# A planned instruction order ranked by lateness over ten passes, with the second projection, the FFN products and the decode buffers moved

## The chip, the cores and the metric

The kernel runs on one core of one Trainium2 chip. The metric is the device time of one execution in microseconds (us), from the median of several runs. The core has five engines that work side by side: PE (matrix multiply; its weight loads are shown apart as PEld), DVE (vector), ACT (scalar and activation), POOL and SP. SP does no arithmetic here: it issues nearly all transfers. Each engine takes its instructions in the order in which the program holds them, and an instruction that waits for another engine holds up what is queued behind it.

## The reference

One step of a hybrid decoder layer, for a prompt of 1024 rows and 8 decode rows of width 1024, with shared weights:

```python
h = x + 0.5 * rmsnorm(swiglu(rmsnorm(x, g1), gate1, up1, down1), p1)   # FFN 1, inner width 2816
proj = rmsnorm(h, g2) @ w_in                  # 1024 -> 3328: q, k, v of group A, the rest group B
ya = diff_attention(q, k, v)                  # 4 heads x 2 maps of 64, causal; decode rows read 512 cached keys
yb, state = rwkv7_time_mix(pb)                # 8 heads of 64, a recurrent state, solved in chunks
h = h + rmsnorm(concat(ya, yb) @ w_out, p2)
h = h + 0.5 * rmsnorm(swiglu(rmsnorm(h, g3), gate2, up2, down2), p3)   # FFN 2
```

Outputs are h for prompt and decode rows, the keys and values, and the states.

## The kernel before, in words

**Tiling.** Rows are the free dimension (columns of the tiles), features lie on the 128 partitions. The 1032 rows are cut in two halves, half 0 with 520 rows (8 decode rows and 512 of the prompt) and half 1 with 512, and each half in two chunks of 256 or 264. Each weight tile is split into a high and a low part in the format fp32r (ACT makes the high part, POOL or DVE the low one), and each product takes three matmuls (`mm3`), high by high, high by low and low by high.

**Stages.** The trunk (`s_trunk`, L751 on) runs four phases: FFN 1 of half 0 (phase 0), FFN 1 of half 1 (phase 1), FFN 2 of half 0 (phase 2) and FFN 2 of half 1 (phase 3). A phase goes through 22 tiles of the inner width; for each tile f there is a gate product, an up product and elementwise work, and after every group of two or three f a down product is added into `y` (tile `xl0`). The activations of four f at most are kept in a ring (tile `xl1`), so after four f a phase cannot go on without a down product, and the first down product waits for `("tail", ph - 1, c)`, the signal that the earlier phase's `y` is read out. Weight tiles of the trunk have four places in phases 0 and 3, and two (`w0`, `w1`) in phases 1 and 2.

Per half, a chain of its own leads from one FFN to the next: `s_tail` (norm of `y`, the residual fetched two tiles at a time into the double buffer `hres`, the sum stored to `res`, its norm, and the input `px` of the projection), `s_project` (26 tiles of w_in), four jobs of the recurrent mixer (`s_job`, two side by side, with locks on shared tiles), `s_attend`, `s_out` (w_out), `s_outnorm` and `s_pre`, which makes the next FFN's input. The decode rows go through `a_decode` (64 gathers of cached pages, issued by POOL: 8 requests, 4 pages, keys and values) and `b_decode`.

**What waits for what around the change.** `s_project(1)` waits for `("outw", 0)`, the end of half 0's output projection. `s_mix(0)` waits for `dec_a` before the jobs may take their sets of tiles, because `a_decode` borrows two of them (`own`). Phase 2 can begin when `s_outnorm` and `s_pre` of half 0 are done, phase 3 when those of half 1 are.

**Order.** The steps are written as streams (generators) that hand in operations. `run` is a list scheduler at build time: it prices each operation with constants in the file (a transfer counts as landed 2.0 us after its bytes, the last line below), keeps a clock for each engine, and again and again takes an operation that can start earliest; among those that can start within 0.02 us of each other the smaller number of the stream's fixed priority (`PRIO`) goes first. On PE the trunk has 3, the projections 1, most others 0. The order so found is the order of the program.

```python
c.append((max(free[e], o.ready + o.load, held[OTHER[e]] if o.port else 0.0), st.prio[e], o))
...
o.seen = rings + 2.0
```

All operations pass through one helper (L277), so the profile tells them apart by their tiles: `trunk_m` is a trunk product, `proj_m` a projection's, `job_aux` and `job_dec` the mixer's, `attn_*` attention's, `out_m` and `outb_m` the output projections of halves 0 and 1, `tail_*` the step between FFN 1 and the projection.

## Time and profile before

| what | us |
|---|---|
| median of 3 runs (2528.1 to 2532.65) | 2532.31 |
| the profiled execution, its own time | 2543.23 |
| span of the profiled execution | 2541.5 |
| PE busy in it | 2368.8 |
| DVE, ACT, POOL busy | 1425.4, 1022.3, 1044.4 |
| mean clock granted to PE, share of full speed | 0.958 |

PE is busy for 93% of the span, no other engine for more than 56%. So the profile is read by stage: where PE is not busy, where its granted clock is under 1.00, and what it waited for there. The time between the profiled execution and its span is 1.7 us.

### The profile page before, as it was taken

Reading aid. Unit: us, or ns where it says so; the run is one execution under the profiler, and the core shown is the slowest. Engines: PE = TensorE matmul, PEld = TensorE weight load, DVE = VectorE, ACT = ScalarE, POOL = GpSimd, SP = SyncE. Lnnn points to the kernel's source line nnn. Section 1 sums busy time; section 2 is a strip of 40 time slices with the busy share of each in tenths; the row PEclk is TensorE's granted clock in tenths of the full one; section 3 lists DMA queues with packets and bytes.
Section 4 is the critical chain, followed back from the end, with each engine's and each line's share of the span. In section 5 each row is a group of like instructions: output and inputs, shape, how many; then the busy total and the mean of one; then the engine's idle time right before and its main releaser. Section 6 shows DMA issues by size and latency. Waiting matters only on the chain.

```text
span 2541.5 us, 41893 instructions
## 1 busy us (share of the span) xinstructions
PE 2368.8 (93%) x16149; PEld 2081.2 (82%) x16149; DVE 1425.4 (56%) x3058; ACT 1022.3 (40%) x1994; POOL 1044.4 (41%) x831
## 2 busy tenths in 40 slices
PE   7999997898999999998499999999999996999998
PEld 7999997698877777776387788989978996788887
DVE  5554444647778676567555367575467656432323
ACT  5632223422244433345444244433365555422223
POOL 4443333435544433355545333343433354322222
PEclk8999999898999999998599999999999998999999
DMA  5422334267653223495355433223444342533232
GB/s 183 130 86 89 92 93 133 73 181 215 195 157 96 84 64 85 111 215 146 96 155 153 141 108 84 80 74 93 107 128 129 112 146 63 157 93 98 88 96 76
DMA packets 455485, 299.14 MB, mean 118 GB/s; under 512 B 79311, under 2 KB 426547, under 8 KB 455286
## 3 DMA queue, kind: packets, MB, share of 16 engines
q1 hardware_dynamic: 449414, 277.55, 37.8%
q0 software_dynamic: 5584, 18.39, 2.4%
q8 instruction: 127, 2.08, 0.3%
q14 instruction: 72, 0.59, 0.1%
q10 hardware_dynamic: 288, 0.52, 0.1%
HBM read 254.91 MB, written 41.49 MB: 117 GB/s over the span
## 4 chain that ended last, share of the span: by engine, by line
PE 73%; DVE 10%; DMA 5%; ACT 5%; POOL 3%; issue 3%; SPq 1%; DVEq 0%; POOLq 0%; ACTq 0%
PE trunk_m L277 45%; PE proj_m L277 8%; PE job_aux L277 6%; PE trunk_aux L277 4%; PE attn_m L277 2%; PE attn_aux L277 2%; PE out_m L277 2%; PE outb_m L277 1%; PE job_dec L277 1%; DVE bset_solve L277 1%; DVE mix_T L277 1%; DVE trunk_xl L277 1%; ACT wts_w L277 1%; POOL wts_w L277 1%; DVE bset_bv L277 1%
## 5 line engine op out<-in xcount | busy, mean ns | idle before, releaser
L277 POOL TENSOR_TENSOR wts_w<-wts_raw,wts_w 128x1024 fp32r<-128x1024 f32 (+1 forms) x183 | 408.0, 2230 | 691.9 <-ACT wts_w L277 603.4
L277 PE MATMUL trunk_m<-pre_X,wts_w 128*128 128x256 f32 (+1 forms) x4224 | 561.7, 290 | 13.1 <-DVE trunk_g L277 8.2
L277 PEld LDWEIGHTS trunk_m<-pre_X,wts_w 128*128 128x128 f32 x4224 | 528.6, 192 | 26.8 <-DVE trunk_g L277 9.0
L277 PE MATMUL trunk_m<-trunk_xl,wts_w 128*128 128x264 f32 (+2 forms) x3105 | 511.4, 318 | 29.8 <-DVE trunk_xl L277 26.0
L277 PEld LDWEIGHTS trunk_m<-trunk_xl,wts_w 128*128 128x128 f32 x3105 | 436.7, 191 | 71.4 <-DVE trunk_xl L277 29.2
L277 PE MATMUL trunk_m<-pre_T,wts_w 128*128 128x512 f32 (+1 forms) x1944 | 453.3, 384 | 2.6 <-DVE wts_w L277 1.3
L277 ACT CAST wts_w<-wts_raw 128x1024 fp32r<-128x1024 f32 (+1 forms) x288 | 281.1, 976 | 392.1 <-PE trunk_m L277 291.9
L277 PEld LDWEIGHTS trunk_m<-pre_T,wts_w 128*128 128x128 f32 x1944 | 340.9, 190 | 75.5 <-issue 7.0
L277 DVE TENSOR_TENSOR trunk_xl<-trunk_xl,trunk_m 128x264 f32<-128x264 f32 (+2 forms) x330 | 158.5, 485 | 151.6 <-PE trunk_m L277 150.3
L277 PE MATMUL proj_m<-tail_X,lin_w 128*128 128x264 f32 (+1 forms) x1248 | 170.0, 296 | 9.7 <-DVE lin_w L277 4.6
L277 PEld LDWEIGHTS proj_m<-tail_X,lin_w 128*128 128x128 f32 x1248 | 162.0, 199 | 19.0 <-ACT tail_X L277 5.4
L277 DVE TENSOR_TENSOR wts_w<-wts_raw,wts_w 128x1024 fp32r<-128x1024 f32 (+1 forms) x105 | 125.5, 1196 | 51.4 <-ACT wts_w L277 50.2
L277 PE MATMUL proj_m<-tail_T,lin_w 128*128 128x512 f32 x624 | 149.3, 398 | 1.9 <-ACT lin_w L277 1.4
L277 PEld LDWEIGHTS proj_m<-tail_T,lin_w 128*128 128x128 f32 x624 | 116.6, 188 | 32.0 <-issue 2.8
L277 POOL TENSOR_TENSOR trunk_xl<-trunk_t,trunk_xl 128x264 fp32r<-128x264 f32 (+2 forms) x84 | 87.1, 1037 | 99.1 <-ACT trunk_xl L277 99.1
L277 DVE SCALAR_TENSOR_TENSOR trunk_g<-trunk_t,trunk_m 128x264 f32<-128x264 f32 (+2 forms) x86 | 45.4, 529 | 124.8 <-ACT trunk_t L277 124.3
L277 ACT CAST trunk_xl<-trunk_t 128x256 fp32r<-128x256 f32 (+2 forms) x136 | 63.8, 469 | 107.7 <-DVE trunk_t L277 67.9
L277 ACT ACTIVATE trunk_t<-trunk_m 128x264 f32<-128x264 f32 (+2 forms) x86 | 40.6, 472 | 142.7 <-PE trunk_m L277 135.7
L277 DVE TENSOR_TENSOR trunk_t<-trunk_g,trunk_m 128x264 f32<-128x264 f32 (+2 forms) x83 | 43.7, 526 | 83.5 <-PE trunk_m L277 78.6
L277 DVE TENSOR_TENSOR bset_solve<-job_LT,bset_solve 128x60 f32<-128x60 f32 (+24 forms) x248 | 80.0, 322 | 17.1 <-DMA job_LT<-Md 7.4
L277 PE MATMUL trunk_aux<-pre_T,wts_w 128*128 128x512 f32 (+1 forms) x360 | 78.9, 374 | 0.0
L277 POOL TENSOR_TENSOR lin_w<-lin_lraw,lin_w 128x1024 fp32r<-128x1024 f32 x20 | 49.2, 2458 | 72.3 <-ACT lin_w L277 61.7
(493 smaller groups left out, 3489.3 us busy)
## 6 DMA issues: line engine op xcount, KB each, us to landing
wts_raw<-in_ffn_gate_dram SPq DMA_DIRECT2D x88, 512.0 KB
wts_raw<-in_ffn_up_dram SPq DMA_DIRECT2D x88, 512.0 KB
wts_raw<-in_ffn_down_dram SPq DMA_DIRECT2D x96, 384.0 KB
lin_lraw<-in_w_in_dram SPq DMA_DIRECT2D x26, 512.0 KB
lin_LT<-in_w_in_dram SPq DMA_DIRECT2D x26, 512.0 KB
wts_raw<-in_ffn_down_dram SPq DMA_DIRECT2D x16, 512.0 KB
lin_lraw<-in_w_out_dram SPq DMA_DIRECT2D x12, 512.0 KB
lin_LT<-in_w_out_dram SPq DMA_DIRECT2D x12, 512.0 KB
```

The costliest lines, as they stand in the source:

```text
L277: o = Op(eng, lambda: fn(*a, **k), st)
```

## The change

The whole order is planned ten times without building it; after each pass `latest` places the operations backward from the planned end and so finds for each the latest start that would not move the end. In the next pass an engine that has several operations ready takes the one with the smallest such number, instead of the stream's priority. The pass with the earliest planned end is built.

Beside that the structure changes. `s_project(1)` no longer waits for half 0's output projection: it gets its own weight places in the tiles of `y` and of the ring (which phase 1 has left), and phase 2 takes these again only after `proj1`. In phase 0 `s_tail` writes its result to two stage tiles and not over `y`, and gives the signal `("tail", 0, c)` there; a new stream `s_resid` fetches the whole residual of a half before `s_tail` needs it, into one of the tiles that held the FFN's input, and these places then take the squares. `px` of chunk 0 now waits for the sums of chunk 1. The decode step has tiles of its own (room for them comes from a smaller `dynamic_dma_scratch_size`), so the jobs do not wait for `dec_a`; `s_out(0)` does. The projection of half 0 begins with the mixer's tiles; that of half 1 does its first two tiles by chunks. A trunk weight is fetched before its place is free, and only the split waits.

```diff
-PRIO = {"stats": (1, 1), "lin": (1, 1), "proj": (1, 1), "tail": (0, 0), "dec": (0, 0), "trunk": (-1, 3), "wts": (0, 0), "outb": (1, 1), "out": (0, 4)}
+PASSES = 10
+
+PRIO = {"stats": (1, 1), "lin": (1, 1), "proj": (1, 1), "tail": (0, 0), "dec": (1, 1), "job": (-2, 0), "trunk": (-1, 3), "wts": (0, 0), "outb": (1, 1), "out": (0, 0), "resid": (-2, 0)}
@@ run
-                        c.append((max(free[e], o.ready + o.load, held[OTHER[e]] if o.port else 0.0), st.prio[e], o))
+                        c.append((max(free[e], o.ready + o.load, held[OTHER[e]] if o.port else 0.0), st.prio[e] if o.late is None else o.late, o))
...
+    def latest(self):
+        late = [self.predicted] * len(self.ops)
+        gaps = {e: [(-1e9, self.predicted)] for e in ENGINES}
+        for i in sorted(range(len(self.ops)), key=lambda i: (self.ops[i].start, i), reverse=True):
+            o = self.ops[i]
+            g = gaps[o.eng]
...
+            t = late[i] = min(b, late[i]) - o.cost
...
+            if o.before is not None:
+                late[o.before] = min(late[o.before], t)
+            for j in o.deps:
+                d = self.ops[j]
+                late[j] = min(late[j], t - o.load - (self.after(d, o) - d.start) + d.cost)
+        return {o.key: t for o, t in zip(self.ops, late)}
@@ s_weights
-                if tag in last:
-                    yield ("wait", last[tag])
                 raw = self.raw()
...
                 nc.sync.dma_start(raw.rearrange("p (a b) -> p a b", a=a), src)
+                if tag in last:
+                    yield ("wait", last[tag])
@@ s_trunk
         for ph in range(4):
+            if ph % 2 == 0:
+                if ph:
+                    yield ("wait", "proj1")
+                y = self.T(self.big, [P, 4160], "xl0")
+                self.ytile, self.y = y, y.rearrange("p (k t) -> p k t", k=KT)
+                ring = self.T(self.big, [P, 4160], "xl1", FR)
@@ s_tail
-        self.post(acc, y, f"n_ffn{1 + ph // 2}_post", h0 + o)
+        z = rs = None
+        if ph < 2:
+            yield ("wait", ("resid", ph))
+            rs = self.rs[c][0]
+        if ph == 0:
+            if c == 0:
+                self.zt = self.stage()
+            z = [a + b for a, b in self.parts(half, *self.zt)][c]
+        self.post(acc, y, f"n_ffn{1 + ph // 2}_post", h0 + o, z, rs)
...
+            if z:
+                self.signal(("tail", ph, c))
...
+            for k in range(KT):
+                nc.scalar.activation(rs[k], y[k], AF.Square)
+                if k:
+                    self.either("tensor_tensor", rb if k > 1 else rb, rb if k > 1 else rs[0], rs[k], ALU.add, engines=("vector",))
+            yield
+            self.rstd(rb)
+            yield
             if c == 0:
+                yield ("wait", ("summed", ph))
                 self.px = self.parts(half, *self.two(half))
...
+            else:
+                self.signal(("summed", ph))
+                yield ("wait", ("px", ph, 0))
@@ new stream, spawned at the last up product of phases 0 and 1
+    def s_resid(self, ph):
+        half = ph % 2
+        yield ("wait", ("ups", ph))
+        yield ("wait", ("loaded", half))
+        t = self.T(self.pool, [P, 4160], f"{'XT'[half]}1")
+        self.rs = self.parts(half, t)
+        t = t.rearrange("p (k t) -> p k t", t=520)
+        for o, n in CHUNKS[half]:
+            a = HALVES[half][0] + o
+            for k in range(0, KT, 4):
+                self.nc.sync.dma_start(t[:, k:k + 4, o:o + n], self.res[:, k:k + 4, a:a + n])
+        self.signal(("resid", ph))
+        yield
@@ s_project
-        yield ("wait", ("outw", 0) if half else "w23")
+        places = None
+        if half:
+            raws, pairs = self.T(self.big, [P, 4160], "xl1"), self.T(self.big, [P, 4160], "xl0", FR)
+            places = [raws[:, 1024 * j:1024 * j + 1024] for j in range(4)], [pairs[:, 2048 * j:2048 * j + 2048] for j in range(2)]
+        else:
+            yield ("wait", "w23")
...
-            list(range(8)) + ms + list(range(8, 12)) + [m + i for i in range(1, 4) for m in job]
+            ms + [m + 1 for m in job] + list(range(8)) + [m + i for i in range(2, 4) for m in job] + list(range(8, 12))
...
-        units = [(i, c) for i in range(len(ms)) for c in ((2,) if half else range(2))]
+        units = [(i, c) for i in range(len(ms)) for c in ((2,) if half and i > 1 else range(2))]
@@ s_out
         if half == 0:
+            yield ("wait", "dec_a")
             yield ("wait", "dec_b")
@@ s_mix
-        if half == 0:
-            yield ("wait", "dec_a")
@@ s_rope
+        if half:
+            yield ("wait", ("outw", 0))
@@ a_decode
-        *self.pages, q0 = [heads(t) for t in [self.own[j][0].rearrange("p n t -> p (n t)") for j in range(2)] + [self.own[j][2] for j in range(2)]]
+        *self.pages, q0 = [heads(self.T(self.pool, [P, HS], f"page{j}")) for j in range(4)]
@@ kernel
-    nc = _bacc.Bacc("TRN2", target_bir_lowering=False, num_devices=1)
+        nc = _bacc.Bacc("TRN2", target_bir_lowering=False, num_devices=1, dynamic_dma_scratch_size=2048)
...
+    for _ in range(PASSES):
+        try:
+            build(late, True)
+        except Planned as p:
+            plans.append((p.args[0], len(plans), late))
+            late = p.args[1]
+    nc = build(min(plans, key=lambda p: p[:2])[2], False)
```

## Rows read from the trace of the kernel before

**Rows 1.** Page, busy us of each engine; and the chain that ended last, by engine.
```profile
PE 2368.8 (93%) x16149; PEld 2081.2 (82%) x16149; DVE 1425.4 (56%) x3058; ACT 1022.3 (40%) x1994; POOL 1044.4 (41%) x831
...
PE 73%; DVE 10%; DMA 5%; ACT 5%; POOL 3%; issue 3%; SPq 1%; DVEq 0%; POOLq 0%; ACTq 0%
```

**Rows 2.** Busy time by stage: window, its us, each engine, PEclk, DMA share, GB/s.
```profile
0.00:64.00 64.00, 48.18 (x326) 45.12 (x327) 32.64 (x64) 34.71 (x64) 31.78 (x34) 0.89 0.55 183
64.00:380.00 316.00, 313.70 (x2597) 312.28 (x2596) 148.54 (x292) 111.02 (x191) 123.77 (x103) 0.99 0.33 98
380.00:510.00 130.00, 104.15 (x647) 92.04 (x647) 68.35 (x110) 53.56 (x94) 52.11 (x55) 0.87 0.35 104
510.00:700.00 190.00, 171.88 (x1302) 164.25 (x1300) 124.50 (x238) 47.85 (x80) 92.47 (x82) 0.95 0.66 196
700.00:1144.00 444.00, 433.41 (x2702) 340.79 (x2702) 305.12 (x761) 183.49 (x372) 191.85 (x136) 0.98 0.44 116
1144.00:1336.00 192.00, 141.91 (x851) 120.18 (x851) 119.57 (x260) 91.17 (x213) 94.76 (x96) 0.80 0.46 133
1336.00:2096.00 760.00, 739.60 (x5657) 659.04 (x5656) 453.37 (x1086) 346.05 (x745) 312.18 (x221) 0.99 0.39 113
2096.00:2160.00 64.00, 43.50 (x306) 40.80 (x306) 43.37 (x71) 35.85 (x66) 29.27 (x34) 0.81 0.21 62
2160.00:2478.00 318.00, 317.28 (x1406) 256.33 (x1405) 105.73 (x139) 93.74 (x124) 97.36 (x57) 1.00 0.36 106
2478.00:2541.50 63.50, 55.16 (x375) 50.33 (x373) 24.20 (x46) 24.82 (x48) 18.88 (x17) 0.95 0.23 75
```

**Rows 3.** Timeline of PE, end of phase 0 [idle before, and its releaser].
```profile
414.78 0.67 PE L277 MATMUL tail_dec<-trunk_acc,init_onesD 128*128 128x264 f32 x2
415.10 7.04 PE L277 MATMUL trunk_m<-trunk_xl,wts_w 128*128 128x256 f32 x57
...
444.47 1.25 PE L277 MATMUL tail_dec<-init_prb,init_onesD 128*128 128x264 f32 x2 [16.01 <-DVE init_prb L277]
449.56 9.24 PE L277 MATMUL proj_m<-tail_X,lin_w 128*128 128x264 f32 x24 [3.84 <-ACT tail_X L277]
...
472.76 17.00 PE L277 MATMUL trunk_m<-pre_T,wts_w 128*128 128x512 f32 x72 [0.86 <-DVE wts_w L277]
```

**Rows 4.** Chain that ended last, inside that wait: start us, us, what.
```profile
429.33 1.15 DVE lin_w L277
430.50 0.37 SPq L277
430.92 4.42 DMA tail_hres<-res
```

**Rows 5.** Timeline of PE, from phase 1's end to the second projection.
```profile
1231.71 2.29 PE L277 MATMUL trunk_m<-trunk_xl,wts_w 128*128 128x256 f32 x9 [6.47 <-DVE trunk_xl L277]
...
1253.41 0.59 PE L277 MATMUL out_m<-out_X,lin_w 128*128 128x264 f32 x1 [15.21 <-ACT out_X L277]
...
1263.62 40.33 PE L277 MATMUL out_m<-out_X,lin_w 128*128 128x256 f32 x335 [0.34 <-DVE out_X L277]
1303.79 2.04 PE L277 MATMUL proj_m<-tail_T,lin_w 128*128 128x512 f32 x8
```

**Rows 6.** Timeline of DVE, last pieces of the second projection's input (tail_T).
```profile
1272.62 0.48 DVE L277 SCALAR_TENSOR_TENSOR tail_T<-tail_sq,setup_cols,tail_T 128x256 fp32r<-128x256 f32 x1 [1.18 <-ACT tail_T L277]
```

**Rows 7.** Page, costliest groups: the two projections (half 0, then half 1) on PE.
```profile
L277 PE MATMUL proj_m<-tail_X,lin_w 128*128 128x264 f32 (+1 forms) x1248 | 170.0, 296 | 9.7 <-DVE lin_w L277 4.6
L277 PE MATMUL proj_m<-tail_T,lin_w 128*128 128x512 f32 x624 | 149.3, 398 | 1.9 <-ACT lin_w L277 1.4
```

**Rows 8.** Timeline of PE, end of the second output projection, and phase 2's end.
```profile
2088.35 5.62 PE L277 MATMUL outb_m<-outb_T,lin_w 128*128 128x256 f32 x46
...
2140.81 9.07 PE L277 MATMUL trunk_m<-trunk_xl,wts_w 128*128 128x264 f32 x55 [14.28 <-DVE trunk_xl L277]
```

**Rows 9.** Chain that ended last, in the decode step: a gather of cached keys.
```profile
560.59 7.59 DMA bset_TT<-in_cache_k_dram,dec_ptab
```

## The prediction, made before the changed kernel ran

> **What bounds the kernel now.** I read the page's busy times and the engine shares of its chain first. PE is busy for 2368.8 us of 2541.5 and carries 73% of the chain; DVE, the next, is busy for 56% [rows 1]. So the kernel ends when PE has done its products, and time can come from three places only: fewer products, less idle time on PE, or less time at its lower clock. The change takes no product away, so I read the second view, busy time by stage, for the other two [rows 2]. Width less PE busy is the idle time of a stage: 15.8, 2.3, 25.9, 18.1, 10.6, 50.1, 20.4, 20.5, 0.7 and 8.3 us, in all 172.7. [...]

> Then I read the waits of PE inside the joints. At the end of phase 0 PE stood 16.01 us before one small product of the tail [rows 3]. The chain of waits says why: the residual's fetch was queued on SP behind a fetch of projection weights, which waited until DVE had split the tile before (429.33 to 430.48); then the fetch took 4.42 us to land [rows 4]. At the end of phase 1 PE stood 6.47 us for DVE, 15.21 us for the input of the output projection, and only at 1303.79, behind 40 us of it, did the second projection begin [rows 5], although the last pieces of its input were made from 1272.62 on [rows 6]. At the end of phase 2 PE stood 14.28 us for a DVE addition that empties its result [rows 8].

> **End of phase 0 (380 to 510): 20 us gained.** Removed: eight residual fetches through the double buffer, with SP's and POOL's share of the wait. Added: four larger fetches issued when the last up product is planned, so they land beside the last down products; the DMA engines are busy for 35% there [rows 2], which covers the same bytes moved earlier. If that cover fails, the fetch costs what it did, about 6 us from 429.33 to its landing at 435.34 [rows 4]. The tail of chunk 0 took from 414.78 to 449.56, 34.8 us [rows 3]; without those 6.0 it takes 28.8. Chunk 1 is some 7 us behind, the 7.04 of its last down products [rows 3], and now holds up the input of both (the wait on the sums): 414.8 + 7 + 28.8 = 451. The first 24 projection products, 3.3 us of work by [rows 7], took 9.24 behind the input's pieces [rows 3], so a chunk of input is worth some 9 us, and both are there by 469. Does PE have work until then? A phase 1 product of 512 columns takes 17.00/72 = 0.236 us [rows 3]; one inner tile has 48 of them, 11.3 us, and four tiles are allowed before the first down product: 45 us from 428 on, to 473. The first down product is allowed early too, since the result no longer lies in `y`. So the 16.0 and the 4.0 of clock go; of the other 9.8 us idle I give back nothing. Bounds: 0, if the wait on the sums puts the hole behind it; 29.9, if all of it goes. I take 20, near the row of the single wait that is named.

> **First projection and decode (510 to 700): 6 us.** The jobs no longer wait for the decode step, and the trunk's early down products can fill. The stage has 18.1 idle and 0.4 of clock, in small waits. No row shows the two side by side; bounds -10 (gathers that land late hold DVE, see the rival) and 18.5. I take a third. Added to it are seven small DVE operations for the decode sums; DVE is busy for 124.5 of 190 us [rows 2] and hides them. Four clears of tiles on POOL go and are worth nothing: POOL is busy for half the stage.

> **End of phase 1 (1144 to 1336): 50 us.** This is the main term. The second projection has 149.3 us of products [rows 7] and did not run while PE stood idle for 50.1 us and lost at least 13.4 to the clock; together 63.5. Its new places are in tiles that phase 1 leaves, so it waits for its own input alone. What is late next is that input: the tail of phase 1, 28.8 us by the count above, when trunk products have ended. Attention of half 0 is the work beside it, if the order keeps some of it until then; the backward plan should, since phase 1's end now heads the longer chain. I leave 13.5 of the 63.5 there. The added wait (phase 2 for `proj1`) has behind it only phase 2's own products, which need half 0's output projection anyway. The second projection's end then lies before the output projection's. Rope of half 1 now waits for that too; attention 1 is what reads it, hundreds of us later. Bounds: 0 and 63.5.

> **End of phase 2 (2096 to 2160): 8 us.** Nothing structural changes. The 14.28 us are an order on DVE and ACT: input of phase 3 ahead of an addition that PE needed [rows 8]. Ranking by the latest start may put the addition first, or move the wait to the input. Bounds 0 and 22.4 (20.5 + 1.9); I take about half of the wait.

> **Elsewhere: nothing.** Start and end (15.8, 8.3) keep their causes, and the stages 700 to 1144 and 1336 to 2096 stand at 97 to 98% PE. The trunk's weights are fetched sooner, with PE waiting for none of them long. Added products: two tiles of the second projection are done by chunks, 96 of 256 columns at 170.0/1248 = 0.136 us for 48 of 512 at 149.3/624 = 0.239 [rows 7], 13.1 - 11.5 = 1.6 us more.

> **Sum.** 20 + 6 + 50 + 8 - 1.6 = 82 us. The profiled execution, 2543.2 with 1.7 outside its span, would come to 2461; the median shown stands 10.9 lower, at 2532.3, so I predict 2450.

> **Rivals.** [...]

> Second, half 1's chain has a length of its own. From its first product at 1303.79 to the last of the output projection at 2094.0 [rows 5, 8] it took 790 us, through four jobs with locks. If PE did not set that, the chain can begin only as early as its input: about 1276 [rows 6], less the 26 us from the first two joints, so 1250, 54 us sooner. Then the gain is 54, at 2480. For it: the trunk fills PE there, at low priority, so that a full PE proves no bound. Against it: with phase 1 ranked ahead of attention its input comes earlier than 1250.

> Third, slower: gathers in order queues. A decode gather on the chain took 7.59 us to land [rows 9]; the order counts 2.0 us after the bytes, so a planned use can be some 5 us early. Now the jobs run beside them with nothing between, and the DVE and POOL instructions behind a late gather are job steps and trunk additions. The 64 gathers at 5 us are 320 us of held queues. The gain is lost when a quarter of it (82/320) reaches PE; at a half the kernel takes 2532 - 82 + 160 = 2610. Against it: with the same gathers beside the first projection PE lost 18.1 us in all [rows 2], and three are in flight at once. [...]

> That the ranking does nothing is possible too, since the first of the ten orders is by fixed priorities and may win: without the 8 and the 6 the time is 2464, inside the forecast.

> **How the numbers follow.** Forecast (2425 to 2475) 0.55; own chain (2475 to 2510) 0.20; clock (2385 to 2425) 0.12; a gain that late landings just eat, 0.04; slower by them, 0.09. A measurement of this kernel tells 0.2% from no change, about 5 us. The range 2400 to 2515 holds the first two and most of the third; it leaves out 0.16. Faster 0.87, same 0.04, slower 0.09.

> **What would show it.** In the changed profile: no wait over 5 us on the residual at the end of phase 0, second-projection products before the first output projection's, and an idle share in the window that answers to 1144 to 1336 of under 20 us. The second rival shows as idle PE before phase 3 with jobs or attention as releasers; the third as gathers releasing DVE or POOL in PE's waits. The prediction is wrong in its main term if PE still stands idle between phase 1's last down product and the second projection.

## The result and the profile after

| | before | after |
|---|---|---|
| median, us | 2532.48 | 2503.59 (4 runs, 2500.17 to 2505.41) |
| ratio, 95% interval | 1 | 0.9877 [0.9859, 0.9896] |
| span of the profiled execution | 2541.5 | 2500.1 |

The change gains 29 us by the medians and 41 by the two profiled spans; the 12 between are the two executions' own, since the profiled one of before lay 10.8 us over its median and that of after 1.6 under. Ratios here and below are of undisturbed executions: e1 had two slow ones, of 2659.26 and 3785.03 us, that its median counts and its ratio does not. 2450 was forecast, a gain of 82. The direction was right, and the time lies inside 2400 to 2515, but the likeliest case is not what happened.

Busy time of the kernel after, from the page, against [rows 1]:

```profile
PE 2375.0 (95%) x16197; PEld 2081.4 (83%) x16197; DVE 1467.3 (59%) x3075; ACT 1009.8 (40%) x1977; POOL 1069.2 (43%) x838
```

DVE does 42 us more in only 17 instructions more, the first hint that something slows it. The stages have moved, so both kernels are read on one set of edges (busy time by stage; columns as in [rows 2]). Before:

```profile
380.00:510.00 130.00, 104.15 (x647) 92.04 (x647) 68.35 (x110) 53.56 (x94) 52.11 (x55) 0.87 0.35 104
510.00:620.00 110.00, 98.17 (x736) 93.80 (x735) 65.23 (x100) 27.36 (x45) 46.82 (x43) 0.92 0.65 195
620.00:1110.00 490.00, 473.65 (x3068) 384.09 (x3068) 340.61 (x826) 183.02 (x347) 220.54 (x163) 0.98 0.45 123
1110.00:1300.00 190.00, 142.35 (x886) 120.13 (x886) 120.49 (x303) 96.06 (x243) 91.71 (x88) 0.79 0.52 139
1300.00:2060.00 760.00, 738.28 (x5540) 652.57 (x5540) 450.91 (x1081) 341.08 (x735) 313.40 (x222) 0.99 0.40 115
```

After:

```profile
380.00:510.00 130.00, 123.03 (x821) 112.63 (x819) 87.36 (x120) 65.06 (x111) 67.94 (x65) 0.97 0.46 137
510.00:620.00 110.00, 110.00 (x916) 109.52 (x916) 34.06 (x59) 27.90 (x44) 30.36 (x18) 1.00 0.49 147
620.00:1110.00 490.00, 442.62 (x2617) 338.53 (x2616) 365.86 (x831) 160.32 (x309) 245.73 (x189) 0.94 0.42 116
1110.00:1300.00 190.00, 159.84 (x953) 135.12 (x952) 143.27 (x323) 107.09 (x262) 104.60 (x91) 0.85 0.63 167
1300.00:2060.00 760.00, 747.91 (x5700) 663.79 (x5698) 474.81 (x1121) 345.69 (x753) 311.54 (x233) 1.00 0.40 117
2060.00:2140.00 80.00, 74.62 (x550) 69.94 (x551) 55.37 (x93) 45.47 (x83) 43.22 (x42) 0.98 0.37 109
```

Width less PE busy is what the reader is to see. The end of phase 0 went from 25.9 us idle to 7.0, the first projection from 11.8 to 0.0. But the stage of half 0's jobs, 620 to 1110, went from 16.4 to 47.4, and its clock from 0.98 to 0.94. At the end of phase 1, 47.7 became 30.2 where I had left 13.5. Second-projection products began no earlier: 1303.30 after, 1303.79 before [rows 5]. Timeline of PE, after, phase 1's last down products to that point:

```profile
1239.82 3.94 PE L281 MATMUL trunk_m<-trunk_xl,wts_w 128*128 128x256 f32 x23
...
1246.01 0.70 PE L281 MATMUL tail_m<-trunk_acc,init_onesD 128*128 128x256 f32 x2 [2.24 <-DVE trunk_acc L281]
...
1279.93 22.14 PE L281 MATMUL out_m<-out_X,lin_w 128*128 128x264 f32 x182
1302.16 1.30 PE L281 MATMUL out_m<-out_X,lin_w 128*128 128x256 f32 x8
1303.30 2.88 PE L281 MATMUL proj_m<-tail_T,proj_xl 128*128 128x256 f32 x23
```

So up to 1303 nothing is gained, and all 41 us of the span lie behind it. What the first two joints gave, the jobs took back. What phase 1's end gave shows as idle time only: up to 1303 PE stood idle for 101.0 us after and 119.8 before, but the same 4920 trunk products were busy for 796.6 us where 775.3 had done. The clock records of both traces hold two values, 1.00 and 0.50 of full speed (before, 1184 to 1261: PEclk 0.50; 1262 to 1343: 1.00). A trunk product of 512 columns (after, `trunk_m<-pre_T,wts_w`) began 0.427 us behind the one before it at 0.50 and 0.233 at 1.00 (medians of 35 and 1336), so that 0.45 of PE's busy time at the lower value is lost; it is counted as a half here, an estimate from these two. Such busy time rose from 99 to 113 us up to 1303, which is 7 of these 21; the rest is not explained.

The products of half 0's jobs begin 86 us earlier (497.0, before 583.4) and end 31 later (1118.8, before 1087.8). Who waits there? The groups of PE with the most idle time before them in 620 to 1110, after (busy, mean ns | idle before, releasers):

```profile
L281 PE MATMUL trunk_m<-trunk_xl,wts_w 128*128 128x512 f32 x409 | 117.0, 426 | 13.6 <-DVE trunk_xl L281 11.6 <-POOL wts_w L281 1.3 <-DVE trunk_t L281 0.7
L281 PE MATMUL job_dec<-mix_T,init_bones 128*128 128x512 f32 x6 | 4.2, 782 | 7.2 <-DVE bset_solve L281 6.8 <-DVE mix_T L281 0.3
L281 PE MATMUL job_dec<-bset_la,bset_wa 64*128 64x512 f32 x12 | 8.6, 806 | 4.9 <-DVE mix_T L281 4.9
```

DVE is the releaser nearly everywhere, though it is busy for only 366 of 490 us. Its timeline, and POOL's, at one such place:

```profile
740.66 0.23 DVE L281 TENSOR_TENSOR bset_solve<-bset_solve 128x72 f32<-128x72 f32 x1
740.93 6.42 DVE L281 TENSOR_TENSOR bset_solve<-job_LT,bset_solve 128x68 f32<-128x68 f32 x1
747.38 0.23 DVE L281 TENSOR_TENSOR bset_solve<-bset_solve 128x68 f32<-128x68 f32 x1
```

```profile
740.48 0.98 POOL L281 DMA_INDIRECT dec_page<-in_cache_k_dram,dec_ptab  x1 [2.36 <-DVE bset_solve L281]
741.48 1.05 POOL L281 TENSOR_TENSOR mix_T<-mix_T 128x512 f32<-128x512 f32 x1
742.48 1.27 POOL L281 TENSOR_TENSOR trunk_xl<-trunk_t,trunk_xl 128x512 fp32r<-128x512 f32 x1
743.70 2.34 POOL L281 TENSOR_TENSOR wts_w<-wts_raw,wts_w 128x1024 fp32r<-128x1024 f32 x1
746.00 1.25 POOL L281 TENSOR_TENSOR dec_page<-dec_page,dec_page 128x512 f32<-128x512 f32 x1
```

A step of the solve that takes 0.23 us took 6.42: it ended when POOL's whole run behind a decode gather had ended, at 747.25.

### The profile page after: what moved, and what is told of

It is laid out like the page before. It is cut to its first block, busy times and chain, and to the rows that moved or that the text cites. A ratio compares the mean times of both kernels' runs of the same rounds, so it can differ in the third digit from the quotient of the medians.

```text
span 2500.1 us, 42004 instructions
## 1 busy us (share of the span) xinstructions
PE 2375.0 (95%) x16197; PEld 2081.4 (83%) x16197; DVE 1467.3 (59%) x3075; ACT 1009.8 (40%) x1977; POOL 1069.2 (43%) x838
## 4 chain that ended last, share of the span: by engine, by line
PE 79%; DVE 13%; ACT 3%; issue 2%; DMA 1%; POOL 1%; SPq 0%; DVEq 0%; ACTq 0%; POOLq 0%
PE trunk_m L281 46%; PE proj_m L281 11%; PE job_aux L281 5%; PE trunk_aux L281 5%; DVE bset_solve L281 3%; PE attn_m L281 2%; PE attn_aux L281 2%; PE outb_m L281 2%; PE out_m L281 2%; PE job_dec L281 1%; DVE trunk_xl L281 1%; DVE mix_T L281 1%; DVE job_st L281 1%; DVE pre_X L281 1%; DVE dec_page L281 1%
## 5 line engine op out<-in xcount | busy, mean ns | idle before, releaser
L281 PE MATMUL trunk_m<-pre_X,wts_w 128*128 128x256 f32 (+1 forms) x4224 | 553.1, 287 | 6.6 <-DVE trunk_g L281 4.8
L281 PE MATMUL trunk_m<-trunk_xl,wts_w 128*128 128x264 f32 (+2 forms) x3105 | 519.1, 319 | 23.6 <-DVE trunk_xl L281 19.6
L281 PE MATMUL trunk_m<-pre_T,wts_w 128*128 128x512 f32 (+1 forms) x1944 | 467.8, 392 | 9.9 <-DVE trunk_g L281 7.4
L281 PEld LDWEIGHTS trunk_m<-pre_T,wts_w 128*128 128x128 f32 x1944 | 349.3, 195 | 86.8 <-DVE trunk_g L281 8.3
L281 PEld LDWEIGHTS proj_m<-tail_X,lin_w 128*128 128x128 f32 x1248 | 151.4, 188 | 4.7 <-issue 2.8
L281 PE MATMUL proj_m<-tail_X,lin_w 128*128 128x264 f32 (+1 forms) x1248 | 153.7, 283 | 0.8 <-DVE tail_X L281 0.8
L281 PE MATMUL proj_m<-tail_T,proj_xl 128*128 128x512 f32 (+1 forms) x672 | 149.0, 381 | 1.4 <-POOL proj_xl L281 1.3
L281 PEld LDWEIGHTS proj_m<-tail_T,proj_xl 128*128 128x128 f32 x672 | 118.8, 188 | 29.7 <-POOL proj_xl L281 2.2
L281 DVE TENSOR_TENSOR bset_solve<-job_LT,bset_solve 128x60 f32<-128x60 f32 (+24 forms) x248 | 102.6, 414 | 8.9 <-ACT bset_TT L281 3.3
L281 DVE TENSOR_TENSOR bset_solve<-bset_solve 128x60 f32<-128x60 f32 (+25 forms) x250 | 80.1, 321 | 4.1
```

What stands on the lines that cost most here:

```text
L281: o = Op(eng, lambda: fn(*a, **k), st)
```

## The experiments

Each run stands beside runs of the kernel before on the same chip; "idle" is width less PE busy, us, from the same windows as above.

| run | us | ratio [95%] | 380-510 | 620-1110 | 1110-1300 | 1300-2140 |
|---|---|---|---|---|---|---|
| before | 2532.5 | 1 | 25.9 | 16.4 | 47.7 | 42.5 |
| after | 2503.6 | 0.9877 [0.9859, 0.9896] | 7.0 | 47.4 | 30.2 | 17.5 |
| e1 structure alone | 2531.0 | 0.9967 [0.9950, 0.9985] | 6.1 | 47.9 | 52.8 | 33.8 |
| e2 ranking alone | 2514.9 | 0.9908 [0.9877, 0.9939] | 25.0 | 17.1 | 51.3 | 32.3 |
| e3 attention held | 2509.3 | 0.9891 [0.9865, 0.9917] | 7.1 | 43.8 | 32.9 | 20.2 |
| e4 POOL first | 2506.1 | 0.9894 [0.9867, 0.9921] | 5.3 | 23.3 | 42.2 | 41.6 |
| e6 thin pages, after | 2472.4 | 0.9759 [0.9712, 0.9806] | 7.5 | 31.8 | 24.1 | 17.6 |
| e7 thin pages, before | 2520.0 | 0.9957 [0.9939, 0.9975] | 26.1 | 11.6 | 51.7 | 39.7 |
| e8 pages on DVE | 2480.3 | 0.9788 [0.9751, 0.9826] | 7.5 | 34.0 | 32.8 | 20.5 |
| e10 gathers marked `port` | 2507.6 | 0.9889 [0.9853, 0.9924] | 7.2 | 29.8 | 38.2 | 39.5 |
| e11 both | 2494.6 | 0.9845 [0.9812, 0.9877] | 7.2 | 30.5 | 48.7 | 25.6 |
| e12 residual late | 2537.3 | 1.0007 [0.9987, 1.0028] | 7.0 | 41.8 | 32.4 | 50.0 |
| e14 eighth order | 2502.3 | 0.9867 [0.9837, 0.9897] | 7.0 | 42.6 | 41.6 | 16.5 |
| e15 fourth order | 2530.8 | 0.9985 [0.9964, 1.0005] | 7.5 | 43.4 | 43.8 | 30.8 |
| e16 weights late | 2511.1 | 0.9897 [0.9858, 0.9937] | 7.8 | 43.7 | 30.7 | 27.0 |
| e17 residual through hres | 2536.4 | 1.0007 [0.9984, 1.0030] | 7.2 | 43.8 | 48.7 | 28.4 |
| e18 pages on DVE, fourth order | 2513.8 | 0.9919 [0.9896, 0.9941] | 7.5 | 43.3 | 34.1 | 29.2 |

The windows come from one execution of each kernel, and these lay between 15.9 us under the kernel's median (e17) and 10.8 over it (before). A few us between two rows are not resolved.

### The two halves of the change: e1 and e2

e1 is the kernel after with a single planning pass, so fixed priorities and the new structure; e2 is the kernel before with the ranking and its ten passes, and none of the structure.

```diff
-PASSES = 10
+PASSES = 1
```

> The changed kernel with one pass, so the structure alone, ordered by the fixed priorities. If the ranking is what moved decode work beside the jobs (theory A: that placement costs some 40 us between 620 and 1110), the structure alone keeps more idle PE at the joints but less in that stage, and comes out at 2490 to 2515, within 15 us of the changed kernel either way. If the 41 us gained behind 1303 come from the ranking (theory C), this kernel gains little over the one before: 2515 to 2535.

> The kernel before with the ten-pass ranking and nothing else. Decode stays beside the first projection, since the jobs wait for it. Theory C (the ranking made the gain behind 1303): 2495 to 2510, as good as the whole change. Rival (the structure made it): 2525 to 2540, no change.

Structure alone gains 8 us (0.0033 of 2535), ranking alone 23, both 29: nearly a sum. Each is one planned order, though, and e14 and e15 below show that orders of one kernel lie up to 28 us apart, so the split into 8 and 23 is not firm. The stages say more. The end of phase 0 closes with the structure (6.1 idle) and not with the ranking (25.0). And the loss among the jobs belongs to the structure as well: every kernel with it has 23.3 or more idle in 620 to 1110, those without it 17.1 at most. The row of 620 to 1110, e1 and then e2:

```profile
620.00:1110.00 490.00, 442.09 (x2712) 337.25 (x2710) 371.12 (x929) 180.34 (x379) 263.70 (x200) 0.95 0.49 131
```

```profile
620.00:1110.00 490.00, 472.89 (x3046) 381.98 (x3045) 346.88 (x841) 186.79 (x360) 229.09 (x166) 0.98 0.45 127
```

One thing that differs there is where the decode step lies. Before, and in e2, the jobs wait for it, and its 64 gathers are issued from 534 to 725 and from 530 to 723, mostly beside the first projection. In e1 they are issued from 560 to 1013, after from 557 to 1033, among the jobs. So the structure spreads them, ranked or not. That the wait for `dec_a` alone does it is not shown: no run puts only that wait back, and e1 also carries the other edits and a later priority for the decode step.

A second thing differs: the first projection ends at 633.2 after and at 694.8 before, so that 99 of its products lie in 620 to 1110 where 489 lay. That is cover which the jobs no longer have. No run holds this apart from the decode step; e6 and the counts below bound what the decode step can have cost.

### The main term, forced: e3 and e4

e3 keeps attention of half 0 back until the second projection's input begins to come; e4 lets POOL go first in the plan when POOL and DVE could start together.

```diff
@@ s_attend
+        if half == 0:
+            yield ("wait", ("px", 1, 0))
@@ run (e4 alone)
-            for e in ENGINES:
+            for e in ("tensor", "gpsimd", "vector", "scalar", "sync"):
```

> The changed kernel, with attention of half 0 held until the input of the second projection is planned, so that phase 1 ends sooner and second-projection products lie beside attention as the prediction had it. If the predicted term is sound and only the order missed it, the idle time of 24 us and the clock loss of some 20 between 1144 and 1336 mostly go: 2465 to 2480. If PE had enough other work there (the rival), no change within 10 us: 2495 to 2515.

> The changed kernel, where the planner lets POOL win when POOL and DVE could start at the same instant, as the trace shows it (a DVE product of 0.22 us took 6.42 us while five POOL instructions ran back to back). Nothing else is edited. Theory A (DVE standing behind runs of POOL instructions is what the order did not count): DVE's busy time falls from 1467 towards 1425, idle PE between 620 and 1110 falls by 20 us or more, and the time is 2460 to 2485. Rival (that stage is short of DVE time whatever the order): DVE busy stays over 1455 and the time is 2495 to 2515.

In e3 the second projection does begin 50 us earlier, at 1253.39, ahead of the output projection:

```profile
1253.39 0.56 PE L281 MATMUL proj_m<-tail_T,proj_xl 128*128 128x256 f32 x1
```

and the stage 1110 to 1300 keeps 32.9 us idle; the whole is no faster than after. Attention had been the cover of phase 1's own end. In e4 attention and the second projection run side by side from 1184.6 on, and the stage has 42.2 idle: phase 1's last trunk products end at 1116.5, and only small products of the jobs, the decode step and attention stand between them and the products that need their result. So the hole moves and doesn't close. e4 does lower the idle time among the jobs to 23.3, and DVE's busy time falls to 1379.8 us, as theory A had it; but it then pays at the end of phase 2, in one wait of the kind that stood there before [rows 8]:

```profile
2106.53 6.49 PE L281 MATMUL trunk_m<-trunk_xl,wts_w 128*128 128x256 f32 x36 [15.11 <-DVE trunk_xl L281]
```

### Is it the decode step's arithmetic? e6 and e7

The order stays as planned; only the call is cut to 8 columns for the products, reductions and sums over pages, once in the kernel after and once in before.

```diff
+        if self.thin:
+            cut = lambda x: x[..., 0:8] if isinstance(x, bass.AP) and x.shape[-1] > 8 else x
+            o.call = lambda: fn(*map(cut, a), **k)
```

> The kernel after with its planned order kept, instruction for instruction, but the decode step's arithmetic on the cache pages (32 products of 128x512, their 32 reductions, and the 128 scaled sums of 128x128 behind them) runs on 8 columns each; all gathers, waits and instruction counts stay. The decode rows of the output are left wrong by that. It takes some 60 us off VectorE and 25 off GpSimd between 640 and 1040. Theory A (the decode work that the ranking moved beside the jobs of half 0 holds VectorE when the solve and the trunk's sums need it): the stage 620 to 1110 falls from 47 us idle and 28 us of clock loss to under 45 together, and the whole to 2465 to 2482. Rival (the stage has too little cover whatever the decode step does, or the clock's loss there has other causes): the stage keeps over 60 us of the 75, and the whole stays over 2490.

> The kernel before with the same cut: order kept, page arithmetic of the decode step on 8 columns (its decode rows of the output are left wrong). There the decode step lies mostly beside the first projection. Theory A: little to gain, 2522 to 2532, since VectorE has room in that stage. Rival (decode arithmetic is a load on the jobs of half 0 in either order): a gain like that of the same cut in the kernel after, 20 us or more.

The same cut is worth 30 us after (0.9877 less 0.9759) and 11 before (0.0043 of 2533). Both are on the theory's side, with 11 a little over the 10 at most that the range for before allowed. So some 19 us are the price of having that arithmetic among the jobs; with the intervals of the three ratios, 5 to 33. It isn't all, and here the theory promised too much: idle time and half of the busy time at the lower clock come to some 54 us in 620 to 1110, where it had under 45 and the rival over 60. Of that stage 31.8 us idle and 49 us at the lower clock remain, against 11.6 and none in the thin kernel before. The gathers themselves are still there.

### What held the 0.23 us product for 6.42: e5, e9, e13

Three probes run behind the last step of the kernel after: POOL does n products of 128x512 back to back, and a DVE product of 64 columns becomes ready at a chosen point. These are the lines of e13; in e9 the activation is missing, and in e5 the head is always a product, whose result DVE's product reads.

```diff
+            put("gpsimd", "tensor_tensor", a, d[:, 0:64], y[:, 0:64], ALU.mult)
+            if head == "gather":
+                put("gpsimd", "indirect_dma_start", t.rearrange("p h e -> p (h e)"), None, ...)
+            else:
+                put("gpsimd", "tensor_tensor", e, e, y[:, 0:512], ALU.mult)
+            for j in range(n):
+                put("gpsimd", "tensor_tensor", x[:, c], x[:, c], y[:, c], ALU.mult)
+            put("scalar", "activation", b, d, AF.Square)
+            put("vector", "tensor_tensor", d[:, 0:64], b[:, 0:64], y[:, 64:128], ALU.mult)
```

> The kernel after, with a probe behind its last step: GpSimd issues 1, 2, 3, 5 or 8 products of 128x512 back to back, and one VectorE product of 64 columns needs only the result of the first of them; once with two operands in SBUF (two), once with one (one), once with one in SBUF and one in PSUM (psum). Theory A (a VectorE product with two operands in SBUF stands behind the whole run of GpSimd instructions, as the one of 6.42 us did): the record of the kind two grows with every GpSimd product queued behind, by about 1.3 us each (some 1.3, 2.6, 5 and 9 us for 1, 2, 4 and 7), while the kinds one and psum stay under 0.5 us. Rival 1 (it waits for one instruction at most): the record of two stays at or under 1.6 us however many are queued. Rival 2 (the 6.42 us came from something else, such as the DMA issue at the head of that run): all records stay near 0.2 us.

> The kernel after with a second probe behind its last step, since the first one showed a VectorE product behind one GpSimd product at a time and never behind the run: GpSimd does a small product, then a head (a 128x512 product, an indirect DMA as the decode step's gathers, or a plain DMA from its queue), then 0, 1, 2, 4 or 7 products of 128x512 back to back; a VectorE product of 64 columns needs the small one only, so it comes due during the head. In the kernel after, the longest VectorE records (6.42, 6.27, 4.31 us) all began inside an indirect DMA's record. Theory A2 (whoever comes due during the indirect DMA stands behind the whole run that follows): with the head a product the record stays at or under 1.5 us; with the indirect DMA it grows by 1.24 us with each product behind, to 5 to 6 us for 4 and 9 us for 7. Whether the plain DMA does the same is open. Rival (the indirect DMA is beside the point, and the long records come from the mix of instruction kinds in those runs): under 1.5 us, or the head's own length, whatever follows.

> A third probe behind the last step of the kernel after. In the second one the VectorE product of 64 columns came due and ran 0.3 us ahead of the indirect DMA's record, so the case in question did not arise. Here it comes due through a 512-column activation on ScalarE, some 0.6 us after GpSimd's small product and so inside the indirect DMA, which took 0.99 to 1.02 us. Theory A2 (who comes due during an indirect DMA stands behind the whole run of products that follows): its record grows by 1.2 us with each product behind: about 0.5, 2, 3, 5.5 and 9 us for 0, 1, 2, 4 and 7, while with a product as head it stays under 1.5 us. Rival: under 1.5 us in both.

e5, timeline of DVE: two operands in SBUF with a run of three POOL products behind the first, then one operand, then one in PSUM:

```profile
2524.97 1.27 DVE L2224 TENSOR_TENSOR probe_page<-probe_page,probe_page 128x64 f32<-128x64 f32 x1 [1.44 <-POOL probe_page L2220]
...
2544.29 1.24 DVE L2226 TENSOR_SCALAR probe_page<-probe_page 128x64 f32<-128x64 f32 x1 [1.44 <-POOL probe_page L2220]
...
2563.32 0.22 DVE L2228 TENSOR_TENSOR probe_page<-probe_page,probe_m 128x64 f32<-128x64 f32 x1 [2.45 <-POOL probe_page L2220]
```

POOL's run went on until 2528.59, yet DVE was through at 2526.24, behind one product of 1.26 us. So theory A in the form "behind the whole run" fell, and I had been wrong too that one operand in SBUF would be free of it. In e9 the DVE product came due and ran 0.3 us ahead of the indirect DMA, so it decided nothing. e13 mended that. Timeline of DVE, with the indirect DMA as head and 0, 1, 2, 4 and 7 products behind:

```profile
2539.04 0.23 DVE L2215 TENSOR_TENSOR probe_page<-probe_page,probe_T 128x64 f32<-128x64 f32 x1 [1.16 <-ACT probe_page L2215]
2543.36 2.03 DVE L2215 TENSOR_TENSOR probe_page<-probe_page,probe_T 128x64 f32<-128x64 f32 x1 [1.16 <-ACT probe_page L2215]
2547.71 0.23 DVE L2215 TENSOR_TENSOR probe_page<-probe_page,probe_T 128x64 f32<-128x64 f32 x1 [1.16 <-ACT probe_page L2215]
2552.56 5.69 DVE L2215 TENSOR_TENSOR probe_page<-probe_page,probe_T 128x64 f32<-128x64 f32 x1 [1.16 <-ACT probe_page L2215]
2559.76 9.32 DVE L2215 TENSOR_TENSOR probe_page<-probe_page,probe_T 128x64 f32<-128x64 f32 x1 [1.16 <-ACT probe_page L2215]
```

and of POOL, the last of these:

```profile
2559.41 0.99 POOL L2215 DMA_INDIRECT probe_page<-in_cache_k_dram,dec_ptab  x1 [0.35 <-issue]
2560.43 8.57 POOL L2215 TENSOR_TENSOR probe_T<-probe_T,probe_T 128x512 f32<-128x512 f32 x7
```

With a product as head the record was 0.60 to 0.61 us in all five cases. Behind the indirect DMA it was 2.03, 5.69 and 9.32, each ending within 0.1 us of the run. The case of two products stayed at 0.23: there it came due only 0.08 us into the DMA (2547.71 against 2547.63), in the others some 0.35. So theory A2 holds with that exception.

In the kernels I counted the DVE records that begin while an indirect DMA runs on POOL and take over 0.5 us more than the lower quartile of their kind (operation, tiles and shape): before 5, with 12.9 us in excess; e2 3 with 6.1; e1 13 with 34.8; after 18 with 55.9, the two longest 6.42 and 6.27. That is the structure's mark again.

### Edits against it: e8, e10, e11, e18

e8 keeps the page products on DVE; e10 gives a gather the mark `port` in the plan, so that a DVE instruction with this mark is placed behind it, as behind a POOL product (e5: 1.27 us with both operands in SBUF, 0.22 with one in PSUM); e11 does both; e18 is e8 built from another of its ten orders.

```diff
-            self.either("tensor_tensor", t, t, qb, ALU.mult)
+            self.either("tensor_tensor", t, t, qb, ALU.mult, engines=("vector",))   # e8, e11, e18
@@ price, a DMA
+            o.port = o.eng == "gpsimd"                                               # e10, e11
```

> The kernel after, but the decode step's 32 products of 128x512 may run on VectorE alone, where 24 of them ran on GpSimd at 1.29 to 1.30 us (0.68 on VectorE); the order is planned anew. Theory A in its narrow form (runs of GpSimd instructions hold VectorE): the stage 620 to 1110 loses 15 to 30 us of its 75, the whole comes to 2480 to 2495. Rival (VectorE is simply short of time in that stage, so that 16 us more of work on it makes it worse): 2503 to 2520.

> The kernel after, planned with each gather (1.04 us in the plan) counted as holding the SBUF port against VectorE, which the plan of after leaves out; so the planner puts no two-operand VectorE instruction beside a gather. Theory A2: the long records in the stage 620 to 1110 get fewer and the stage loses 10 to 25 us of its 75; whole 2480 to 2497. Rival (the planner only knows of a wait then, and has no other place to put the work; or another order opens another hole): 2497 to 2515.

> Both edits: page products on VectorE alone, and gathers counted as holding the port in the plan. Theory A2, with the two effects partly the same time: 2465 to 2482, under the 2480.33 of the page products alone. Rival (the gain of the page products was the luck of one order of work): 2482 to 2510.

> The page products on VectorE alone (2480.33 us with its fifth order), built from its fourth order, whose planned end is 4.2 us later. Theory (fewer GpSimd runs behind indirect DMAs help whichever order is taken): 2475 to 2497, under the kernel after. Rival (that gain was one good order out of a spread of some 30 us, as the fourth and the sixth order of the kernel after showed): 2497 to 2530.

e8 came to 2480.33 us (2474.58 to 2485.35), under both kernels; its interval doesn't meet that of after. But e18, the same edit in an order that the plan holds nearly equal, took 2513.82, so the rival holds: e8's gain is in good part its order. e10 took 17.6 us of idle time from the jobs and gave it back behind 1110 (38.2 and 39.5, after 30.2 and 17.5), and e11, forecast under e8, lies 14 us over it. No edit of this kind is shown to help by itself. Fourth order against fourth, and each plan's best against best, the page edit is 17 and 23 us faster (e18 and e15, e8 and after), but two pairs of differently planned orders show no more than a hint.

The edits bound the theory, too. Counted as above, e10 has 6 long records with 15.5 us in excess and e11 2 with 4.1, about what the kernel before has, and still they keep 29.8 and 30.5 us idle in 620 to 1110. So, as far as these orders compare, DVE behind POOL's runs is worth some 17 of the 31 us that this stage lost, at most. Their gain there goes with more trunk products in it (1455 and 1450, after 1177), and phase 1 is then spent sooner: of their idle time in 1110 to 1300, 23.6 and 30.5 us lie before products of the jobs.

### How much is the order: e14 and e15

```diff
-    nc = build(min(plans, key=lambda p: p[:2])[2], False)
+    nc = build(plans[7][2], False)      # e15: plans[3][2]
```

> The kernel after in all its structure and rules, built from its eighth order instead of its sixth; by the plan the two ends lie 1.5 us apart. Theory A (the place of the decode step and the rules of the ranking set the loss in the stage 620 to 1110, and any of the late orders has it): 2495 to 2512, with 60 to 90 us idle and lost to the clock in that stage. Rival (the loss belongs to the one order that was taken; orders that the plan holds equal differ on the chip by 15 us or more): outside that band on either side, with the losses in other stages.

> The same from the fourth order, whose planned end lies 2.6 us behind the one taken. Theory A: 2495 to 2512. Rival (spread of equal plans): outside that band; with the eighth and the sixth order it gives the spread of three.

Three orders of one kernel, whose planned ends lie within 2.6 us: 2503.59, 2502.30 and 2530.84. The spread is as large as the whole gain. The three share the loss among the jobs (47.4, 42.6, 43.4 idle), so theory A is right about that; where the fourth order falls behind is later, 30.8 against 17.5 and 16.5 in 1300 to 2140.

### What closed the end of phase 0: e12, e17, e16

```diff
-        yield ("wait", ("ups", ph))
+        yield ("wait", ("sum", ph, 0, KT - 1))                         # e12, s_resid
-        self.post(acc, y, ..., h0 + o, z, rs)
+        self.post(acc, y, ..., h0 + o, z, rs if ph else None)          # e17, s_tail
+                if tag in last:
+                    yield ("wait", last[tag])                          # e16, ahead of the fetch again
```

> The kernel after with one wait put back: the residual rows are fetched only behind phase 0's last product, as in the kernel before, instead of ahead of the end of phase 0; the order is planned anew. Theory (the fetch of the residual was the wait that ended last at the end of phase 0): the idle time of 380 to 510 goes from 7 back to 17 to 26 us, the whole to 2510 to 2525. Rival (with a free product buffer the wait for it is covered by the trunk's other work): idle of 380 to 510 stays under 12 us, whole 2495 to 2510.

> The kernel after with the residual of phase 0 fetched as before, two tiles at a time through the double buffer hres, from inside the tail; all else stays, the order is planned anew. The prediction named this fetch as what held PE at the end of phase 0. Theory: the idle time of 380 to 510 goes from 7 back to 17 to 26 us. Rival (phase 1's products, whose weights are fetched earlier and whose results no longer wait, cover the tail whatever the fetch takes): idle of 380 to 510 stays under 12 us. The whole may move by 30 us either way with the new order, as the late residual showed, so the stage decides.

> The kernel after with the wait of the trunk's weights put back ahead of their fetch, as in the kernel before; all else stays, the order is planned anew. Neither the late residual nor the fetch through hres opened the end of phase 0 again (7.0 and 7.2 us idle in 380 to 510). Theory: in the kernel before phase 1's first products lacked their weights there, and the earlier fetch is what closed it; then the idle time of 380 to 510 goes back to 15 to 26 us. Rival: it stays under 12 us, and no single edit of these three did it. The whole moves with the new order, by up to 30 us either way, so the stage decides.

Idle time of 380 to 510: 7.0, 7.2 and 7.8. None of the three opens it again, but two of the edits hardly moved there what they were to move. The timeline of SP has phase 0's residual fetch, after and then e12:

```profile
397.58 2.55 SPq L281 DMA_DIRECT2D resid_X<-res  x4
```

```profile
397.43 2.23 SPq L281 DMA_DIRECT2D resid_X<-res  x4
```

The fetch is no later in e12. It is phase 1's that the edit moves, from 1170.94 to 1208.85, since `s_resid` serves both phases. In e16 the trunk's weight fetches between 380 and 470 are issued within 3 us of those of after, 12 of them where after has 13 and before 7. Only e17 does what it says: its fetches go through `hres` again, yet its second pair is issued at 421.2, where it stood until 430.9 before [rows 4]. So that roundabout road does not open the end of phase 0; a late fetch was not tried. That the structure as a whole closes it is shown by e1; which edit does so stays open.

The whole of e12 and e17 is 33 us slower than after, in e12 outside what was expected either way. In e17 that comes from stages that the edit doesn't touch, as in e15. In e12 it can't be told apart from the later fetch of phase 1; an 18.62 us wait of the second tail stands there:

```profile
1308.15 1.22 PE L281 MATMUL tail_m<-init_prb,init_onesD 128*128 128x256 f32 x2 [18.62 <-DVE init_prb L281]
```

## Why the prediction was right or wrong

The stages can be added up as idle time plus half of the time in which PE was busy at the lower clock (0.50), both counted from the traces. The end of phase 0 gave 22.7 us where 20 were forecast, the first projection (510 to 620) 19.8 and the jobs (620 to 1110) minus 49.4 where the forecast had 6 and nothing, the end of phase 1 12.6 where it had 50, the end of phase 2 16.4 where it had 8. The rest of the span gave 28.1, where nothing was forecast. That makes 50.2 for the 41.4 of the spans; 8.8 are not explained.

**End of phase 0, 20 us: right in size, unproven in cause.** Idle time fell by 18.9 and the time at the lower clock from 34 us to 7. I said that the fetch of [rows 4] was to blame and that without it the tail of chunk 0 takes 28.8 us; with the fetch early it took 38.1 (407.98 to the first projection product at 446.05), longer than the 34.8 before, and with the fetch back on its old road (e17) the gain stayed. The hole closed because phase 1's products cover the tail, not because the tail became shorter.

**First projection and decode, 6 us, bounds -10 and 18.5: the step that failed.** I weighed the stage 510 to 700, where the decode step lay, and not the one it would move into. The near part did gain: idle 11.8 to 0.0 in 510 to 620. But 620 to 1110 lost 31.0 us of idle time, and 41 us more of it ran at the lower clock. "Elsewhere: nothing" for 700 to 1144 was the same mistake, since a stage at 97% PE is one in which DVE has no room to be held up: it was busy for 305 of 444 us with a solve whose steps follow each other.

**End of phase 1, 50 us: failed.** I forecast 13.5 us of idle and clock loss and the second projection ahead of the output projection; 30.2 us idle remain, with 58 us at the lower clock (some 45 of them with PE busy), and the products began at 1303.30. The step that failed is "attention of half 0 is the work beside it": phase 1's tail and the second projection's input both need cover, and there is one attention. e3 and e4 placed it at either end, for nothing. The order of the two projections is not the cause: in e4, e10 and e11 the second begins first, at 1184.6, 1173.9 and 1197.9, and 42.2, 38.2 and 48.7 us stay idle. My own sign for a wrong main term, PE idle between phase 1's last down product and the second projection, is what the rows show.

**End of phase 2, 8 us: more than that, by another road.** Idle time in 2060 to 2140 fell from 20.7 to 5.4. I gave this to the ranking; e2 has 17.8 there, e1 6.9. That points to the structure, but e4, with all of it, has 25.7: the order can undo it. Which edit does it I didn't try.

**Rivals.** That the ranking does nothing was wrong: alone, in the one order built, it gains 23 us, over the 14 I gave it, and the structure 8 where I gave it 68. Half 1's own chain was wrong in its premise: from its first projection product to its last output product it took 747.7 us (1303.30 to 2050.95) where 790 stood, and all of the gain is there. Nor does an earlier start bring it forward: begun 119, 129 and 105 us sooner in e4, e10 and e11, it ended at 2064.3, 2059.3 and 2045.6. Slower by gathers had the place and the engines right, jobs and trunk sums behind DVE and POOL, but not the mechanism: idle time of DVE and POOL that a landed page ended is small (9.0 us, before 31.1); part of the cost is that DVE is shut out while POOL runs on (18 records with 55.9 us in excess, before 5 with 12.9). The clock gave back next to nothing: some 214 us at the lower clock became about 140 (mean clock 0.958 before, 0.972 after), but that is mostly time in which PE was idle. With PE busy it was 125 us before and 119 after, worth 62 and 59, since a new stage fell to it. The sums of the forecast use 4.0, 0.4, 13.4 and 1.9 us of loss to the clock, which no run shows: in 380 to 510, 510 to 700, 1144 to 1336 and 2096 to 2160 of before PE was busy for 14, 20, 36 and 10 us at 0.50, worth 7, 10, 18 and 5 at a half.

**What I left out** is the spread of orders. The forecast took each joint as a mechanism with a price and gave the sum 25 us to either side. A list order of some 42000 instructions adds about 30 us that no joint shows, so even with the right terms that band was too narrow.

## What to carry to other kernels

When a step is let loose from a wait, price it in the stage it can drift into, on the engine that is the latency path there, and not in the stage it leaves. Work that covers one hole is not there for the next: count the cover before you count the hole as gone. And where an order comes out of a planner, build two or three of its near-equal plans before a gain of one per cent is put down to an edit. When an edit is to bring a cause back, look in the trace whether it moved what it was to move, before its result counts for or against.

## What the runs showed of the hardware

Two things were unexpected. In e5 a DVE product of 64 columns waited for the POOL product that was running (1.27 us with two operands in SBUF, 1.24 with one, 0.22 with one operand in PSUM), but got in behind that one: it was through at 2526.24, and POOL's run at 2528.59.

In the trace of before the 3048 records of DVE arithmetic and the 1829 of ACT stand one for one in the order of the program.
